# An earlier first weight chunk, other pauses around an inverse, and one bank for the last sums in a single-core layer

## The chip, the cores and the metric

The kernel runs on one core of one Trainium2 chip. Five engines of the core take part: TensorE (PE in the profile) multiplies matrices, VectorE (DVE), ScalarE (ACT) and GpSimd (POOL) work on tiles, and SyncE (SP) sends DMAs. ScalarE sends DMAs too, from a queue of its own. Each engine takes its instructions in a fixed order, and a wait stops what stands behind it on the same engine. The metric is the time of one execution on the device in microseconds. Before the change it is 2013.53 us, the median of three runs (2012.96 to 2017.21).

## The reference

One layer is computed for 256 prompt tokens and 8 single-token samples, 264 columns in all (T), at a model width of 2048 (16 tiles of 128):

```
x = x + 0.5 * swiglu(rmsnorm(x), gate1, up1, down1)     # width 5504 = 43 tiles
p = rmsnorm(x) @ w_in                                   # 38 tiles of 128 columns
mix = [ rwkv7(p[r, k, v, w, a, g]), attention(p[q, k, v]) ]   # 16 heads of 64 each
x = x + mix @ w_out
x = x + 0.5 * swiglu(rmsnorm(x), gate2, up2, down2)
y = rmsnorm(x)
```

The RWKV part runs a recurrence over the tokens, `S = S*decay - (S kk)(kk a)^T + v k^T`. The attention part is a window of 128 with a sink and a relative bias; the samples use cached keys and values. States and new cache rows are outputs beside y.

## The kernel before

**Weights.** Each weight matrix comes as chunks of 128 x 512 in float32. `chunk()` (L116) makes a raw tile by DMA on SP (256 KB; six raw buffers), then a rounded copy hi on ScalarE (L123) and lo = raw - hi on VectorE (four buffers each). TensorE takes hi and lo in `gemm` (L127): per 128 x 128 block three matmuls of 264 columns, hi by the high part of the activations, hi by their low part, lo by the high part, so 12 per chunk. There are 1288 chunks: 1 to 536 are the first feed-forward part, 537 to 688 w_in, then w_out and the second feed-forward part. The numbers of chunks in the prediction count these.

**The start.** Ten matmuls on a tile of ones (NWARM) run before any data is there. `first_ffn` (L285 on) loads x0 (the norm's gains and tile 0 of x) and the next tiles of x on ScalarE's queue; `load(k)` splits tile k into its high and low part. In the first part of `ffn` eight banks are filled in turns of four k-tiles.

**The mixing stage.** The w_in product runs over 38 tiles with `tick` after every chunk (and the w_out product too). A tick advances all living tasks by one step; tasks are generators, and `pause(n)` lets n ticks pass. So the program's order interleaves small work with chunks. A planner (the tile framework with a timeline of its own) then fixes each engine's order from that, with the chunks' casts and subtractions at high priority, and it may move work past other work of the same engine. RWKV runs in four batches of two head pairs. `prep` makes the scaled keys, gates and the masked products gm of a pair; `chain` (L521) does the rest of a batch:

1. blocks of gm go through DRAM (sa) to X and Y, 32 x 32 triangles (tile name Xt for Y), in the layout of L539 and L540;
2. `pause(DWAIT[i])`, then a 30-step inverse on VectorE, two small operations per step (st and Xt);
3. the inverse goes through DRAM again, sb by L557 and TT by L562, on SP;
4. `pause(DWAIT[i])`, then two VectorE transposes, TN (L567);
5. matmuls TN,gm, a ScalarE copy zs (L579), matmuls TT,zs, a copy into TT (L588), matmuls kr,TT, copies W (L602) and uv (L604);
6. matmuls of W, uv, and the recurrence of three S steps, each followed by VectorE updates Z and S; then y copied from the bank (L657) and from XD (L658), S sent out from ScalarE's queue (out_wkvp, L660), and a norm (matmuls y,C, squares, t,C, reciprocals L693).

```
yield from pause(DWAIT[bt.i])
for s in range(1, 31):
    ...
    tt(V, t, bc(X[:, s:s + 1, s + 1:], shp), bc(Y[:, :m, s:s + 1], shp), ALU.mult)
    tt(V, Y[:, :m, s + 1:], Y[:, :m, s + 1:], t, ALU.add)
...
yield from pause(DWAIT[bt.i])
TN = ring((P, n * 4, 32), "TN", 1)
```

Attention tasks (scores, softmax, the product with the values) start after the RWKV batches have been launched and run between the same chunks.

**The tail.** `second_ffn` collects squares of the finished x tiles into two sums. At the end matmuls turn each sum into a column of a bank (sm), two columns of three are added, a square root and a reciprocal follow, three matmuls spread the factor over 128 partitions (rp), ScalarE copies it to rb, and VectorE (from rp) and GpSimd (from rb) multiply the 16 tiles, each piece going out by DMA in turn on SP and ScalarE's queue (L952). Five matmuls into `hot` follow the sums.

Of the kernel before, what the change touches and what calls it, by code (L numbers as in the profile page):

```python
# [9 lines left out]
AF = mybir.ActivationFunctionType  # L10
ALU = mybir.AluOpType
# [16 lines left out]
CH, NRAW, NHL = 4, 6, 4  # L28
NACC, NM = 3, 5
NS, NO, NY, NH, NT, NLD = 38, 8, 8, 40, 16, 6  # L30
NWARM = 10
NGM, NKR, NUV, NTT, NBT = 10, 5, 3, 2, 5
NSTEP = 4
DWAIT = (8,8,8,4)
PW = (2, 1, 3, 2, 9)
ALPHA = math.exp(-0.5)
LKV = 26
# [10 lines left out]
def body(tc, I, O):  # L48
# [8 lines left out]
    def tt(e, out, a, b, op):  # L57
        return e.tensor_tensor(out=out, in0=a, in1=b, op=op)  # L58
# [8 lines left out]
    def act(out, in_, f, **k):  # L67
        return A.activation(out=out, in_=in_, func=f, **k)  # L68
# [4 lines left out]
    def mm(out, lhsT, rhs, start=True, stop=True, **k):  # L73
        TE.matmul(out, lhsT, rhs, start=start, stop=stop, **k)  # L74
# [20 lines left out]
    with ExitStack() as ctx:  # L95
# [17 lines left out]
        def mp():  # L113
            return pp.tile([P, 512], F32, tag="m", bufs=NM, name=uid("m"))
# [9 lines left out]
                tt(e, lo[:, :w], raw[:, :w], hi[:, :w].bitcast(F32), ALU.subtract)  # L124
            return hi, lo

        def gemm(ps, src, xs, step=None, rng=None, ahead=True):  # L127
            n = len(xs)
            for k0 in range(0, n, CH):
                k1 = min(n, k0 + CH)  # L130
                if rng and k0 not in rng:
                    continue
                hi, lo = chunk(src[:, k0 * P:k1 * P], k1 - k0, V, ahead)
                for k in range(k0, k1):
                    xh, xl = xs[k]
                    c = slice((k - k0) * P, (k - k0 + 1) * P)
                    mm(ps[:, :T], hi[:, c], xh, k == 0, False)
                    mm(ps[:, :T], hi[:, c], xl, False, False)
                    mm(ps[:, :T], lo[:, c], xh, False, k == n - 1)
                if step:  # L140
                    step()
# [65 lines left out]
            n, c, b = copies.pop()  # L207
            tc.keep_in_program_order(A.dma_start(O[n][b, 0:127, :], I[c][b, 1:128, :]))

        def ffn(nrm, xr, gu, dn, nxt, load, begin=None, side=None):  # L210
            rstd = None
            f0 = 0
            for pi, nf in enumerate(PARTS):
                hs = [None] * nf
                late = []
                if begin:
                    early(pi)
                first = pi == 0
                if first:
                    banks = [acc() for _ in range(NACC)] + [mp() for _ in range(NM)]  # L220
                    n0 = len(banks) // 2
                    for k in range(CH):
                        at = load(k)
                    for k0 in range(0, KD, CH):
                        if begin and k0 + CH < KD:
                            begin(k0 // CH + 1)
                        xs = nrm.xs + [None] * (KD - len(nrm.xs))
                        for i, ps in enumerate(banks):
                            with tc.issue_after(at.ins) if begin and k0 == 0 < i else nullcontext():
                                gemm(ps, gu[i // 2, i % 2], xs, rng=(k0,), ahead=False)  # L230
                            if i >= len(banks) - CH and k0 + CH < KD:
                                load(k0 + CH + i - len(banks) + CH)
                    for f in range(n0):
                        raw = [tmp(), tmp()]
                        V.tensor_copy(raw[0], banks[2 * f][:, :T])
                        A.copy(raw[1], banks[2 * f + 1][:, :T])
                        late.append((f, *raw))
                for f in range(f0 + n0 if first else f0, f0 + nf):
                    pgu = [acc(), acc()]
                    if first and f == n0:  # L240
                        sq = iter(range(KD))

                        def step():
                            for k in [x for _, x in zip(range(2), sq)]:
                                nrm.square(xr[k], k % 2, True)
                    else:
                        step = None
                    if begin and pi and copies:
                        copy_one()
                    if side and pi:  # L250
                        next(side, None)
                    for ps, w in zip(pgu, (gu[f, 0], gu[f, 1])):
                        gemm(ps, w, nrm.xs, step)
                    last = f == f0 + nf - 1
                    if rstd is None:
                        rstd = nrm.rstd(tmp())
                    late.append((f, *(x[:, :T] for x in pgu)))
                    now = [late.pop()]
                    for _ in range(len(late) if last else min(len(late), 2 if first and f == n0 + 1 else 1)):
                        now.append(late.pop(0))  # L260
                    for j, pg, pu in now:
                        E = V if last else G
                        g = tmp()
                        tt(V, g, pg, rstd, ALU.mult)
                        s = tmp()
                        act(s, g, AF.Silu)
                        u = tmp()
                        tt(V, u, pu, rstd, ALU.mult)
                        tt(E, u, u, s, ALU.mult)
                        hi, lo = tmp(dt=F32R), tmp(dt=F32R)  # L270
                        A.copy(hi, u)
                        tt(E, lo, u, hi.bitcast(F32), ALU.subtract)
                        hs[j - f0] = (hi, lo)
                if pi == len(PARTS) - 1:
                    nrm.xs = None
                for o in range(KD):
                    ps = acc()
                    gemm(ps, dn[o, :, f0 * P:(f0 + nf) * P], hs)
                    stt(xr[o], ps[:, :T], 0.5, xr[o], ALU.mult, ALU.add)
                    if pi == len(PARTS) - 1:  # L280
                        nxt(o)
                f0 += nf

        def first_ffn(n2):
            def load(k0):  # L285
                return n1.split(xr[k0], True)

            def nxt(o):
                n2.split(xr[o])
                n2.square(xr[o])  # L290
                A.dma_start(xsp[o], xr[o])

            with tc.tile_pool(name="f1", bufs=1) as fp:
                cur[0] = (fp, NH)
                x0 = fp.tile([P, KD + T], F32, name="x0")
                A.dma_start(x0, I["x0"])
                n1 = Norm(VG1, gains=x0[:, 0:KD])
                xr = [x0[:, KD:]]
                for j0, j1 in ((1, 2), (2, 4)):
                    xg = fp.tile([P, j1 - j0, T], F32, name=uid("x"))  # L300
                    A.dma_start(xg, I["xT"][:, j0:j1, :])
                    xr += [xg[:, j] for j in range(j1 - j0)]

                def more(q):
                    xg = fp.tile([P, 4, T], F32, tag="x", bufs=3, name=uid("x"))
                    tc.keep_in_program_order(A.dma_start(xg, I["xT"][:, q * 4:q * 4 + 4, :]))
                    xr.extend(xg[:, j] for j in range(4))

                ffn(n1, xr, I["gu1"], I["dn1"], nxt, load, more)

        def dec_state(fp, XR):
            n = 4
# [599 lines left out]
        def second_ffn(n3, xr, XR):  # L912
# [6 lines left out]
            with tc.tile_pool(name="f2", bufs=1) as fp:  # L919
# [11 lines left out]
                ffn(n3, xr, I["gu2"], I["dn2"], nxt, load, None, side)  # L931
                assert next(side, side) is side
                p = fin.sums[0]
                sm, rp, hot = [mp(), mp()], mp(), mp()
                for m, q in zip(sm, p):
                    for j in range(3):
                        mm(m[0:88, j:j + 1], q[:, j * 88:j * 88 + 88], ones[:, 0:1])
                for _ in range(5):
                    mm(hot[:, :P], ones, p[1][:, :P])
                A.copy(rt[:, 3:6], sm[0][0:88, 0:3])  # L940
                tt(V, rt[:, 0:3], sm[1][0:88, 0:3], rt[:, 3:6], ALU.add)
                act(rt[:, 0:3], rt[:, 0:3], AF.Sqrt, scale=1.0 / D, bias=eps[0:88, 0:1])
                V.reciprocal(rt[:, 0:3], rt[:, 0:3])
                for j in range(3):
                    mm(rp[:, j * 88:j * 88 + 88], bc(rt[:, j:j + 1], (88, P)), C[0:88, CID:CID + 88])
                rb = tmp()
                A.copy(rb, rp[:, :T])
                for i, (e, o, n) in enumerate(((V, 0, 1), (V, 1, 1), (G, 2, 1), (V, 4, 4), (G, 3, 1), (V, 8, 4), (G, 14, 1), (V, 12, 2), (V, 15, 1))):
                    y = ys[o // 4][:, o % 4:o % 4 + n]
                    r = rb if e is G else rp[:, :T]  # L950
                    tt(e, y, y, bc(r.unsqueeze(1), (P, n, T)), ALU.mult)
                    (SP, A)[i % 2].dma_start(O["yT"][:, o:o + n, :], y)  # L952
# [109 lines left out]
```

## Time and profile before

| | before |
|---|---|
| median of 3 runs (lowest, highest) | 2013.53 us (2012.96, 2017.21) |
| the profiled execution's time | 2014.05 us |
| its span | 2012.1 us |
| mean granted TensorE clock | 0.997 |
| TensorE busy | 1990.5 us (99%) |
| VectorE busy | 1306.4 us (65%) |
| ScalarE busy | 1032.6 us (51%) |
| GpSimd busy | 257.0 us (13%) |
| DMA moved | 358.39 MB, 178 GB/s over the span |

Rows of a timeline begin with the start and the length in us; then stand the engine, the line, the operation, out<-in, the shape and the number of merged instructions; in square brackets, the idle time before and what released it. Matmul records count twice for float32 operands (ten matmuls are twenty rows). In the answers on waits there are the total, the number and the longest, in us. PEclk is the share of full clock that TensorE was granted.

### The profile page before, as it was taken

Reading aid. Unit: us, or ns where it says so; the run is one execution under the profiler, and the core shown is the slowest. Engines: PE = TensorE matmul, PEld = TensorE weight load, DVE = VectorE, ACT = ScalarE, POOL = GpSimd, SP = SyncE. Lnnn points to the kernel's source line nnn. Section 1 sums busy time; section 2 is a strip of 40 time slices with the busy share of each in tenths; the row PEclk is TensorE's granted clock in tenths of the full one; section 3 lists DMA queues with packets and bytes.
Section 4 is the critical chain, followed back from the end, with each engine's and each line's share of the span. In section 5 each row is a group of like instructions: output and inputs, shape, how many; then the busy total and the mean of one; then the engine's idle time right before and its main releaser. Section 6 shows DMA issues by size and latency. Waiting matters only on the chain.

```text
span 2012.1 us, 45443 instructions
## 1 busy us (share of the span) xinstructions
PE 1990.5 (99%) x17088; PEld 1956.4 (97%) x17088; DVE 1306.4 (65%) x2576; ACT 1032.6 (51%) x2047; POOL 257.0 (13%) x368
## 2 busy tenths in 40 slices
PE   9999999999999999999998999999999999999998
PEld 9999999999999999999988889999999999999998
DVE  5865555655556577688777766776666666666665
ACT  5644444444444456655555654654444444444445
POOL 0401001010010222121200010120101001010012
PEclk9999999999999999999999999999999999999999
DMA  6565565655555566554555345565565665655554
GB/s 226 177 192 193 183 194 189 185 184 176 187 177 185 182 200 211 153 157 129 149 150 165 118 137 181 174 184 184 192 179 191 187 192 189 185 191 184 191 179 145
DMA packets 227708, 358.39 MB, mean 178 GB/s; under 512 B 42384, under 2 KB 81312, under 8 KB 227488
## 3 DMA queue, kind: packets, MB, share of 16 engines
q1 hardware_dynamic: 220896, 346.41, 55.0%
q10 hardware_dynamic: 6592, 9.08, 1.4%
q8 instruction: 134, 2.20, 0.4%
q14 instruction: 86, 0.70, 0.1%
HBM read 347.26 MB, written 10.21 MB: 178 GB/s over the span
## 4 chain that ended last, share of the span: by engine, by line
PE 94%; DMA 2%; DVE 2%; issue 1%; ACT 1%; SPq 1%; DVEq 0%; POOL 0%; ACTq 0%; POOLq 0%
PE acc L74 85%; PE m L74 8%; DMA sb<-Xt 1%; DVE lo L58 0%; DMA TT<-sb 0%; DMA xsp<-x 0%; DMA x<-in_x 0%; DMA Xt<-sa 0%; PE m L507 0%; ACT t L68 0%; DVE y L58 0%; DMA sa<-gm 0%; SPq L557 0%; ACT hi L123 0%; PE m L757 0%
## 5 line engine op out<-in xcount | busy, mean ns | idle before, releaser
L58 DVE TENSOR_TENSOR lo<-raw,hi 128x512 fp32r<-128x512 f32 (+1 forms) x1288 | 871.2, 680 | 547.9 <-ACT hi L123 521.1
L123 ACT CAST hi<-raw 128x512 fp32r<-128x512 f32 (+1 forms) x1288 | 777.1, 607 | 840.9 <-PE acc L74 762.3
L74 PE MATMUL acc<-s,hi 128*128 128x264 f32 x5940 | 1112.0, 287 | 0.9 <-ACT hi L123 0.9
L74 PEld LDWEIGHTS acc<-s,hi 128*128 128x128 f32 x5940 | 924.2, 189 | 6.7 <-issue 1.9
L74 PE MATMUL acc<-s,lo 128*128 128x264 f32 x2970 | 848.9, 286 | 4.1 <-DVE lo L58 3.9
L74 PEld LDWEIGHTS acc<-s,lo 128*128 128x128 f32 x2970 | 560.3, 189 | 8.0 <-DVE lo L58 5.4
L74 PE MATMUL acc<-t,hi 128*128 128x264 f32 x2752 | 502.6, 284 | 0.0
L74 PEld LDWEIGHTS acc<-t,hi 128*128 128x128 f32 x2752 | 426.0, 188 | 0.0
L74 PE MATMUL acc<-t,lo 128*128 128x264 f32 x1376 | 388.6, 284 | 0.0
L58 POOL TENSOR_TENSOR t<-t,t 128x264 f32<-128x264 f32 (+1 forms) x148 | 150.9, 1020 | 1148.3 <-ACT hi L123 790.8
L74 PEld LDWEIGHTS acc<-t,lo 128*128 128x128 f32 x1376 | 258.3, 188 | 0.0
L74 PE MATMUL acc<-y,hi 128*128 128x264 f32 x648 | 123.7, 284 | 0.0
L74 PEld LDWEIGHTS acc<-y,hi 128*128 128x128 f32 x648 | 100.9, 188 | 0.1
L74 PE MATMUL acc<-y,lo 128*128 128x264 f32 x324 | 91.7, 283 | 0.0
L58 DVE TENSOR_TENSOR t<-acc,t 128x264 f32<-128x264 f32 x156 | 67.4, 432 | 36.8 <-PE acc L74 36.5
L58 POOL TENSOR_TENSOR o<-o,o 128x264 f32<-128x264 f32 x43 | 36.4, 847 | 234.6 <-ACT o L68 228.9
L74 PE MATMUL acc<-o,hi 128*128 128x264 f32 x324 | 63.1, 285 | 0.0
L74 PEld LDWEIGHTS acc<-y,lo 128*128 128x128 f32 x324 | 61.0, 188 | 0.0
L61 DVE SCALAR_TENSOR_TENSOR s<-acc,s 128x264 f32<-128x264 f32 x96 | 40.6, 427 | 15.4 <-PE acc L74 14.9
L74 PEld LDWEIGHTS acc<-o,hi 128*128 128x128 f32 x324 | 50.3, 188 | 0.0
L74 PE MATMUL m<-s,hi 128*128 128x264 f32 x260 | 48.0, 284 | 0.0
L61 DVE SCALAR_TENSOR_TENSOR x<-acc,x 128x264 f32<-128x264 f32 x96 | 40.5, 426 | 9.8 <-PE acc L74 9.3
(249 smaller groups left out, 1278.8 us busy)
## 6 DMA issues: line engine op xcount, KB each, us to landing
raw<-in_gu SPq DMA_DIRECT2D x688, 256.0 KB, 3.3
raw<-in_dn SPq DMA_DIRECT2D x224, 256.0 KB, 2.8
raw<-in_win SPq DMA_DIRECT2D x152, 256.0 KB, 3.4
raw<-in_dn SPq DMA_DIRECT2D x160, 192.0 KB, 2.7
raw<-in_wout SPq DMA_DIRECT2D x64, 256.0 KB, 3.2
xsp<-x ACTq DMA_DIRECT2D x16, 132.0 KB, 3.7
s<-xsp SPq DMA_DIRECT2D x16, 132.0 KB, 4.2
ld<-in_sT SPq DMA_DIRECT2D x16, 128.0 KB, 3.5
```

The source lines that it names most:

```text
L58: return e.tensor_tensor(out=out, in0=a, in1=b, op=op)
L61: return V.scalar_tensor_tensor(out=out, in0=a, scalar=s, in1=b, op0=op0, op1=op1)
L74: TE.matmul(out, lhsT, rhs, start=start, stop=stop, **k)
L123: A.copy(hi[:, :w], raw[:, :w])
```

## The change

There are three parts. At the start, one more warm-up matmul is made; tile 0 of x is split and the first weight chunk (raw, hi, lo) is made before the other tiles of x are asked for; and the load of tiles 2 and 3 of x (264 KB) goes to SP's queue, behind that first chunk's, instead of being the third on ScalarE's. `gemm` and `ffn` take the ready chunk. In the mixing stage, the pauses of `chain`, which stand both ahead of the inverse and between its end and the transposes, are 10, 10, 10 and 2 instead of 8, 8, 8 and 4. At the tail, the six matmuls of the two sums add into one bank, so that the copy and the addition are gone; there are three hot matmuls instead of five; the factor for GpSimd comes from a second bank with three matmuls of its own; and the 16 tiles are cut into eight pieces instead of nine, with two for GpSimd (tiles 8 and 12) instead of three (2, 3 and 14).

```diff
-NWARM = 10
+NWARM = 11
-DWAIT = (8,8,8,4)
+DWAIT = (10,10,10,2)
...
-        def gemm(ps, src, xs, step=None, rng=None, ahead=True):
+        def gemm(ps, src, xs, step=None, rng=None, ahead=True, ready=None):
...
-                hi, lo = chunk(src[:, k0 * P:k1 * P], k1 - k0, V, ahead)
+                hi, lo = ready or chunk(src[:, k0 * P:k1 * P], k1 - k0, V, ahead)
...
-                    for k in range(CH):
+                    for k in range(len(nrm.xs), CH):
                         at = load(k)
...
-                                gemm(ps, gu[i // 2, i % 2], xs, rng=(k0,), ahead=False)
+                                gemm(ps, gu[i // 2, i % 2], xs, rng=(k0,), ahead=False, ready=ready)
+                            ready = None
...
-                for j0, j1 in ((1, 2), (2, 4)):
+                at = load(0)
+                with tc.issue_after(at.ins):
+                    first = chunk(I["gu1"][0, 0][:, 0:CH * P], CH, V, False)
+                for e, j0, j1 in ((A, 1, 2), (SP, 2, 4)):
                     xg = fp.tile([P, j1 - j0, T], F32, name=uid("x"))
-                    A.dma_start(xg, I["xT"][:, j0:j1, :])
+                    e.dma_start(xg, I["xT"][:, j0:j1, :])
...
-                sm, rp, hot = [mp(), mp()], mp(), mp()
-                for m, q in zip(sm, p):
+                sm, rp, hot = mp(), mp(), mp()
+                for i, q in enumerate(p):
                     for j in range(3):
-                        mm(m[0:88, j:j + 1], q[:, j * 88:j * 88 + 88], ones[:, 0:1])
-                for _ in range(5):
+                        mm(sm[0:88, j:j + 1], q[:, j * 88:j * 88 + 88], ones[:, 0:1], i + j == 0, i == 1, skip_group_check=True)
+                for _ in range(3):
                     mm(hot[:, :P], ones, p[1][:, :P])
-                A.copy(rt[:, 3:6], sm[0][0:88, 0:3])
-                tt(V, rt[:, 0:3], sm[1][0:88, 0:3], rt[:, 3:6], ALU.add)
-                act(rt[:, 0:3], rt[:, 0:3], AF.Sqrt, scale=1.0 / D, bias=eps[0:88, 0:1])
+                act(rt[:, 0:3], sm[0:88, 0:3], AF.Sqrt, scale=1.0 / D, bias=eps[0:88, 0:1])
                 V.reciprocal(rt[:, 0:3], rt[:, 0:3])
...
-                rb = tmp()
-                A.copy(rb, rp[:, :T])
-                for i, (e, o, n) in enumerate(((V, 0, 1), (V, 1, 1), (G, 2, 1), (V, 4, 4), (G, 3, 1), (V, 8, 4), (G, 14, 1), (V, 12, 2), (V, 15, 1))):
+                rb, again = tmp(), mp()
+                for j in range(3):
+                    mm(again[:, j * 88:j * 88 + 88], bc(rt[:, j:j + 1], (88, P)), C[0:88, CID:CID + 88])
+                A.copy(rb, again[:, :T])
+                for i, (e, o, n) in enumerate(((V, 0, 1), (V, 1, 1), (V, 2, 2), (V, 4, 4), (G, 8, 1), (V, 9, 3), (G, 12, 1), (V, 13, 3))):
```

More of the change, by code (lines that the diff above doesn't have):

```diff
@@ L208, in copy_one, with ffn @@
             tc.keep_in_program_order(A.dma_start(O[n][b, 0:127, :], I[c][b, 1:128, :]))
-        def ffn(nrm, xr, gu, dn, nxt, load, begin=None, side=None):
+        def ffn(nrm, xr, gu, dn, nxt, load, begin=None, side=None, ready=None):
             rstd = None
@@ L307, in more @@
                     xr.extend(xg[:, j] for j in range(4))
-                ffn(n1, xr, I["gu1"], I["dn1"], nxt, load, more)
+                ffn(n1, xr, I["gu1"], I["dn1"], nxt, load, more, None, first)
         def dec_state(fp, XR):
```

## The prediction

> **What bounds the kernel now.** I read the page first, then the waits of TensorE, then the timeline around each wait. The page says that little but TensorE can be shortened:
>
> ```profile
> span 2012.1 us, 45443 instructions
> PE 1990.5 (99%) x17088; PEld 1956.4 (97%) x17088; DVE 1306.4 (65%) x2576; ACT 1032.6 (51%) x2047; POOL 257.0 (13%) x368
> ```
>
> Only some 21 us of the span are without a matmul. No part of the change removes a large matmul, so it can only move those 21 us, or the speed at which matmuls run. The waits of TensorE (line, releaser, total, times, longest) say where they are:
>
> ```profile
> PE acc L74 <- DVE lo L58: 3.9, 3, 2.2
> PE m L74 <- ACT zs L579: 3.5, 1, 3.5
> PE m L74 <- ACT W L602: 1.4, 1, 1.4
> PE m L74 <- DVE TN L567: 0.5, 1, 0.5
> ```
>
> All four lie in the mixing stage, where the pauses work. The largest, in the timeline of TensorE, with the ScalarE copy that ends it and the same matmuls of an undisturbed batch (914):
>
> ```profile
> 1094.14 0.69 PE L74 MATMUL m<-TN,gm 32*32 32x32 f32 x32
> 1098.29 1.45 PE L74 MATMUL m<-TT,zs 32*32 32x32 f32 x32 [3.45 <-ACT zs L579]
> 1101.25 3.73 PE L74 MATMUL m<-kr,TT 64*64 64x128 f32 x32
> ...
> 1097.87 0.75 ACT L579 COPY zs<-m 32x256 f32<-32x256 f32 x2
> ...
> 914.42 1.97 PE L74 MATMUL m<-kr,TT 64*64 64x128 f32 x32
> ```
>
> The reader sees a stop of 3.45 us in batch 3, then matmuls at nearly twice their time (3.73 against 1.97). The windows show why (columns: window, length, five engines, PEclk, DMA share, GB/s):
>
> ```profile
> 1098.00:1102.00 4.00, 3.56 (x48) 3.00 (x49) 1.82 (x9) 2.78 (x10) 0.00 (x0) 0.58 1.04 343
> 1102.00:1106.00 4.00, 4.00 (x34) 3.67 (x32) 2.53 (x12) 3.99 (x16) 0.74 (x1) 0.56 0.89 284
> 1037.80:1044.00 6.20, 6.17 (x62) 5.80 (x64) 6.20 (x13) 3.14 (x6) 2.14 (x5) 1.00 0.63 167
> ```
>
> For 8 us the clock was 0.57, which costs 8 x 0.43 = 3.4 us; after a stop of 2.20 in batch 2, at 1037, it stayed at 1.00. Batch 3 thus pays 3.45 + 3.4 = 6.9 us.
>
> **The pauses, batch 3 (4 to 2).** In the instruction order of the changed kernel the last inverse step of batch 3 stands after lo 682 (chunks counted from the start), the transposes after lo 686 and 688, and ScalarE copies zs before the softmax's exponentials instead of behind them. Between TN,gm and TT,zs stand about 20 weight matmuls. The 6.9 us go. Late next are W and uv, whose copies stand behind casts and softmax work; the nearest row is the W wait of 1.4. I take 2.0 for new waits (bounds 0 and 6.9): **-4.9**.
>
> **The pauses, batches 0 to 2 (8 to 10).** Here the pause stands twice, ahead of the inverse and between its end and the transposes. But it counts chunks as the program is written, and the planner puts the transposes nearer: the inverse of batch 1 ends after lo 623 and both transposes stand between lo 624 and 625; in batch 2 the end is after lo 652, the transposes on both sides of the work behind lo 655; in batch 0 the end is after lo 608, the transposes behind lo 611 (before: 612 and 613). What the way through DRAM takes, from VectorE's timeline of batch 1 and batch 2:
>
> ```profile
> 944.25 0.16 DVE L58 TENSOR_TENSOR Xt<-Xt,st 128x8 f32<-128x8 f32 x1
> ...
> 952.65 0.43 DVE L567 STREAM_TRANSPOSE TN<-TT 32x256 f32<-32x256 f32 x1 [2.16 <-DMA TT<-sb]
> ...
> 1023.05 0.17 DVE L58 TENSOR_TENSOR Xt<-Xt,st 128x8 f32<-128x8 f32 x1
> ...
> 1033.76 0.43 DVE L567 STREAM_TRANSPOSE TN<-TT 32x256 f32<-32x256 f32 x1 [2.47 <-DMA TT<-sb]
> ...
> 1037.83 0.40 PE L74 MATMUL acc<-s,lo 128*128 128x264 f32 x1 [2.20 <-DVE lo L58]
> ```
>
> From the end of the inverse to the first transpose it is 8.4 us (952.65 - 944.25) or 10.7, and the transpose was waiting already. While it waits, VectorE makes no lo, and TensorE has at most four chunks in hand. The prices for the rest, from the page (lo, in ns) and the timelines:
>
> ```profile
> L58 DVE TENSOR_TENSOR lo<-raw,hi 128x512 fp32r<-128x512 f32 (+1 forms) x1288 | 871.2, 680 | 547.9 <-ACT hi L123 521.1
> ...
> 912.82 0.62 ACT L123 CAST hi<-raw 128x512 fp32r<-128x512 f32 x1 [0.55 <-PE acc L74]
> 914.28 0.62 ACT L123 CAST hi<-raw 128x512 fp32r<-128x512 f32 x1 [0.85 <-PE acc L74]
> ...
> 915.70 0.21 DVE L58 TENSOR_TENSOR st<-X,Xt 128x50 f32<-128x50 f32 x1
> 919.52 1.79 DVE L422 RECIPROCAL t<-m 128x264 f32<-128x264 f32 x1
> ...
> 925.96 1.07 ACT L458 COPY uv<-m 64x128 f32<-64x128 f32 x4 [0.66 <-PE m L455]
> 935.21 0.34 ACTq L660 DMA_DIRECT2D out_wkvp<-S  x1
> 936.62 0.61 PE L74 MATMUL m<-y,C 128*128 128x264 f32 x2
> ...
> 953.13 0.37 ACT L510 COPY BT<-m 128x256 f32<-128x256 f32 x1 [0.21 <-PE m L507]
> 953.51 0.74 ACT L512 COPY BT<-m 64x256 f32<-64x256 f32 x2
> ```
>
> A chunk is 1.46 us (914.28 - 912.82). Batches 0 and 1 meet at chunks 617 to 625; I count from the end of the second S step on TensorE, in 617, as 0.
> First wait: before the update that the third S step needs (chunk 619), VectorE now has 12 inverse operations (2.5), two mask multiplies and lo 621 of 512 columns (2.0) and some five small ones (0.9, an estimate at 0.2 each): ready at 5.4 less the 0.6 that the second step itself takes, 4.8. TensorE is there after two chunks, 2.9: **1.9**.
> Second wait: TensorE reaches the second y,C in chunk 621 at 4.8 + 3.8 = 8.6 (two chunks and 0.9 of small work after the step). The last S is ready at 7.7 (lo 622 and ten small operations later), and ScalarE's queue now holds, ahead of the second y<-XD copy, the DMA issue of S that waits for it (0.34), four kr copies (1.07), one of 0.37, another issue (0.34) and three BT copies (1.1): 11.1. **2.5**.
> Third wait: the inverse ends at 9.8 (0.2 + lo 623 + six steps after that S), so TN is at 18.2 at the soonest; with 0.43, a reciprocal of 1.79 between the transposes, the second transpose 0.43 and lo, lo 625 is there at 21.5 to 22. TensorE goes on at 11.1, has the rest of 621 and 622 to 624 (5.7) and some nine small matmuls at 0.3 (2.7), and wants lo 625 at 19.7: **2.2**.
> Together 6.6 where the old order lost 0.2 (the waits of lo, 3.9 in three, less batch 2's 2.2, lie elsewhere): **+6.4**. Bounds: 0, if TensorE is itself late by these few us, and 11 if lo 621 comes late too.
> Batch 2 has the same ScalarE order in chunk 651 while y,C stands in 649: the same count gives 3.0. Its transposes hold lo 656: the inverse ends 9.4 after its third S step, TN is 8.4 to 10.7 later, two reciprocal-sized pieces and small ones (3.6) follow to lo 656: 22 to 24 against TensorE's 19.5, 2.5 to 4.5, say 3.1 where it was 2.2. **+3.9** (bounds -2.2 and +7).
> Batch 0: TN,gm stands 1.7 chunks earlier, 2.5 us; the row shows 0.5 now and VectorE's spare time takes part: 1.5. **+1.0** (0 to 2.5).
>
> **The start.** The first chunk, x0 and the loads, in the timeline:
>
> ```profile
> 0.99 4.63 PE L74 MATMUL m<-ones 128*128 128x128 f32 x20 [0.99 <-POOL eps L150]
> 6.56 0.81 PE L74 MATMUL acc<-s,hi 128*128 128x264 f32 x2 [0.94 <-ACT hi L123]
> 7.95 0.51 ACT L68 ACTIVATE s<-x,x 128x264 fp32r<-128x264 f32 x1 [1.02 <-DMA x<-in_xT]
> 12.73 0.64 PE L74 MATMUL acc<-s,hi 128*128 128x264 f32 x2
> 13.33 0.40 PE L74 MATMUL m<-s,hi 128*128 128x264 f32 x2
> ```
>
> SP takes the 264 KB of xT[2:4] between the first weight chunk and the second, ScalarE's queue loses it, and ScalarE no longer waits 1.02 for it. The eleventh warm-up matmul costs 4.63 / 10 = 0.46 (the ten are 20 rows) inside the 0.94 of waiting. Behind it, raw 1 and later come 0.6 later on SP; six chunks in hand hide that. **-1.0** (bounds +0.3, and -3 if the half-speed pairs, 0.64 against 0.40, end one stretch earlier).
>
> **The tail.**
>
> ```profile
> 2000.61 0.63 PE L74 MATMUL m<-ones,o 128*88 128x1 f32 x6 [0.65 <-ACT o L68]
> 2001.10 1.36 PE L74 MATMUL m<-o,ones 128*128 128x128 f32 x10
> 2001.34 0.16 DVE L58 TENSOR_TENSOR rt<-m,rt 88x3 f32<-88x3 f32 x1 [1.30 <-PE m L74]
> 2003.13 0.38 ACT L947 COPY t<-m 128x264 f32<-128x264 f32 x1 [1.30 <-PE m L74]
> 2003.54 4.05 DVE L58 TENSOR_TENSOR y<-y,m 128x264 f32<-128x264 f32 x6 [1.51 <-ACT t L947]
> 2003.59 2.14 POOL L58 TENSOR_TENSOR y<-y,t 128x264 f32<-128x264 f32 x3 [4.70 <-ACT t L947]
> ```
>
> The sum of two banks goes (0.16). VectorE need not wait for the copy (2003.54 - 2003.13 = 0.4). Each of five hot matmuls is 0.27 (1.36 / 5); two fewer count where the factor's matmuls stand behind them, and I count half, 0.3. Against these 0.9, GpSimd starts later behind three more matmuls and its copy, with two tiles instead of three, and the last piece is three tiles (396 KB) where it was one: 0.4. I take **-0.5** (bounds -0.9, and +0.5 if that last transfer is the end).
>
> **Sum.** -1.0 - 0.5 + 1.0 + 6.4 + 3.9 - 4.9 = +4.9. The profiled run took 2014.05 (1.95 around its span), 0.52 above the median of three, 2013.53; from the median it is 2018.4. I call a change under 0.2% (4.0 us) none, about what this kernel's measurement can tell.
>
> **Rivals.**
> A, the forecast: new waits in batches 0 to 2 exceed what batch 3 saves. 2016 to 2022; 0.40, of which 0.10 below 2017.6.
> B, faster: TensorE, not VectorE, is behind at each end of the inverse, so that VectorE is four chunks ahead when it meets the transposes. Four chunks and their small matmuls are 5.8 + 2.7 = 8.5, as much as the 8.4 of the loads: it decides if VectorE has that lead at lo 624 and 655. Batch 1 before speaks for it (VectorE waited 2.16, TensorE not at all), batch 2 against it. Then only batch 3's saving and the ends count, with 0 to 2 of small waits: 2013.5 - 1.5 - 6.9 + 1.0 = 2006. 0.25.
> C, slower still: the new stops cut the clock as at 1098. There 3.45 us did it, while the 2.20 of batch 2 left it at 1.00. Stops of 3 and 3.1 are near that; one more such loss gives 2018.4 + 3.4 = 2022, two 2025. 0.17. The Trainium skill, "TensorE: Matmul & The Clock Gate", section "Why this matters for your kernels", says to leave no idle gap of TensorE over about 3 us, since an idle window halves the clock; by that rule the stops of 3.0 and 3.1 would both be charged and the time be 2025. The trace agrees for 3.45.
> D, the pauses do nothing net: half of the waits are hidden, 2018.4 - 5 = 2013. 0.18, nearly all within 0.2%.
> So faster 0.26 (B and a little of D), within 0.2% 0.27, slower 0.47. Range 2006 to 2026.
>
> **What would show it.** TensorE's waits of the changed kernel: zs gone and PEclk 1.00 near 1094; waits for lo, for y's copy and for S between 915 and 945, and two in batch 2; VectorE's wait of TN for TT<-sb above its total of before. At the start, no wait of ScalarE for xT; at the tail, VectorE's first product some 0.7 us nearer to the last square. Wrong, if TensorE waits under 3 us in batches 0 to 2, or if a half-clock stretch remains after batch 3's transposes.

## The result, and the profile after

The changed kernel takes 1998.72 us, the median of five runs (1997.52 to 2000.81), against 2013.53 before (2008.44 to 2017.21, five runs). The ratio is 0.9929, with a 95% interval from 0.9912 to 0.9947: some 14 us less, where 5 us more were forecast. The forecast range began at 2006.

The head of the page of the changed kernel:

```profile
span 1996.9 us, 45460 instructions
PE 1983.0 (99%) x17092; PEld 1952.0 (98%) x17092; DVE 1305.6 (65%) x2575; ACT 1030.9 (52%) x2046; POOL 258.6 (13%) x367
```

and its waits of TensorE (line, releaser, total, times, longest):

```profile
PE m L74 <- DVE TN L571: 1.2, 1, 1.2
PE acc L74 <- DVE lo L58: 1.0, 4, 0.3
PE m L74 <- DVE y L58: 0.4, 1, 0.4
PE acc L74 <- POOL s L58: 0.3, 1, 0.3
```

TensorE stands still for 13.9 us (21.6 before), and is busy for 7.5 us less with the same large matmuls. The waits for zs, for W and the 2.2 us for lo are gone. (Lines behind the start have moved by three or four: L571 is the old L567.)

Three reciprocals (L194) stand at the same place of the work in both kernels: the norm of the first feed-forward part, the norm ahead of w_in, and that of the second feed-forward part. Their rows in the timeline of VectorE cut the span into stages. Before:

```profile
71.04 1.80 DVE L194 RECIPROCAL t<-t 128x264 f32<-128x264 f32 x1 [0.63 <-ACT t L68]
...
774.47 1.80 DVE L194 RECIPROCAL rs<-rs 128x264 f32<-128x264 f32 x1 [1.03 <-ACT rs L68]
...
1304.66 1.80 DVE L194 RECIPROCAL t<-t 128x264 f32<-128x264 f32 x1 [0.48 <-ACT t L68]
```

and after:

```profile
67.94 1.80 DVE L194 RECIPROCAL t<-t 128x264 f32<-128x264 f32 x1 [0.62 <-ACT t L68]
...
771.29 1.80 DVE L194 RECIPROCAL rs<-rs 128x264 f32<-128x264 f32 x1 [1.02 <-ACT rs L68]
...
1290.78 1.80 DVE L194 RECIPROCAL t<-t 128x264 f32<-128x264 f32 x1 [0.43 <-ACT t L68]
```

The start gives 3.1 us (71.04 - 67.94), the rest of the first feed-forward part 0.1, the stretch with the mixing stage 10.7 (530.19 to 519.49), and what follows 1.3 (707.44 to 706.12). The sum is the 15.2 us of the two spans. In the mixing stage TensorE stands still for 2.8 us where it stood for 9.8; the other 3.7 us of the 10.7 are time in which it was busy.

**The mixing stage.** The last step of the inverse and the first transpose of batch 1 (931) and of batch 3 (1068), with batch 3's matmuls, in the timelines of VectorE and TensorE of the changed kernel:

```profile
931.62 0.17 DVE L58 TENSOR_TENSOR Xt<-Xt,st 128x8 f32<-128x8 f32 x1
...
938.12 0.43 DVE L571 STREAM_TRANSPOSE TN<-TT 32x256 f32<-32x256 f32 x1 [3.13 <-DMA TT<-sb]
...
1068.92 0.17 DVE L58 TENSOR_TENSOR Xt<-Xt,st 128x8 f32<-128x8 f32 x1
...
1077.86 0.43 DVE L571 STREAM_TRANSPOSE TN<-TT 32x256 f32<-32x256 f32 x1 [3.68 <-DMA TT<-sb]
1078.34 0.24 PE L74 MATMUL m<-TN,gm 32*32 32x32 f32 x2 [1.16 <-DVE TN L571]
...
1088.49 1.96 PE L74 MATMUL m<-kr,TT 64*64 64x128 f32 x32
```

Batch 3 now costs 1.16 us and keeps its clock (kr,TT takes 1.96, not 3.73). VectorE does wait for a transpose, 3.13 and 3.68 us, as was forecast; but TensorE does not come to a stop behind it in batch 1.

**The start.** The first matmul into a bank of tag m in TensorE's timeline of the changed kernel:

```profile
10.26 0.41 PE L74 MATMUL m<-s,hi 128*128 128x264 f32 x2
```

It runs at 10.26, at 13.33 before: the stretch of pairs that took 0.64 is not there.

**The tail.** VectorE's first product and the sums ahead of it:

```profile
1985.59 0.63 PE L74 MATMUL m<-ones,o 128*88 128x1 f32 x6 [0.64 <-ACT o L68]
1987.71 4.33 DVE L58 TENSOR_TENSOR y<-y,m 128x264 f32<-128x264 f32 x6 [0.99 <-PE m L74]
```

The product starts 2.12 after the last sums, 2.93 before, and from those sums to the end of the span it is 11.3, against 11.5: VectorE's 0.8 is lost again behind it, for from the first product to the end of the span it is 9.2, against 8.6.

### The profile page after: what moved, and what is told of

It is laid out like the page before. It is cut to its first block, busy times and chain, and to the rows that moved or that the text cites. A ratio compares the mean times of both kernels' runs of the same rounds, so it can differ in the third digit from the quotient of the medians.

```text
span 1996.9 us, 45460 instructions
## 1 busy us (share of the span) xinstructions
PE 1983.0 (99%) x17092; PEld 1952.0 (98%) x17092; DVE 1305.6 (65%) x2575; ACT 1030.9 (52%) x2046; POOL 258.6 (13%) x367
## 4 chain that ended last, share of the span: by engine, by line
PE 97%; DMA 1%; DVE 1%; issue 0%; ACT 0%; SPq 0%; POOL 0%; DVEq 0%; ACTq 0%; POOLq 0%
PE acc L74 87%; PE m L74 9%; DVE lo L58 0%; PE m L511 0%; DMA TT<-sb 0%; DMA xsp<-x 0%; DMA sb<-Xt 0%; DMA x<-in_x 0%; DVE y L58 0%; DMA Xt<-sa 0%; PE m L761 0%; PE m L498 0%; DMA ld<-in_g 0%; PE m L763 0%; PE m L762 0%
## 5 line engine op out<-in xcount | busy, mean ns | idle before, releaser
L61 DVE SCALAR_TENSOR_TENSOR s<-acc,s 128x264 f32<-128x264 f32 x96 | 40.6, 427 | 15.5 <-PE acc L74 15.1
```

What stands on the lines that cost most here:

```text
L61: return V.scalar_tensor_tensor(out=out, in0=a, scalar=s, in1=b, op0=op0, op1=op1)
```

## The experiments

Each is the kernel before with a part of the change, or the changed kernel with one number moved. The ratios are to the kernel before, in runs of the same chip.

**The start alone.**

```diff
-NWARM = 10
+NWARM = 11
...
+                at = load(0)
+                with tc.issue_after(at.ins):
+                    first = chunk(I["gu1"][0, 0][:, 0:CH * P], CH, V, False)
+                for e, j0, j1 in ((A, 1, 2), (SP, 2, 4)):
```

> The kernel before with the start part alone (eleven warm-up matmuls, first chunk made ahead, tiles 2 and 3 of x on SP's queue). Theory 1 (each part acts by itself, and the sum of the parts is the change): the full-speed pairs begin about 3 us earlier, at about 10.3 instead of 13.3, and the time falls by 3.0 us (2 to 4); the waits of the mixing stage stay as they were before, zs 3.5, lo of batch 2 2.2, W 1.4. Theory 2 (an earlier start shifts the loads of the mixing stage against each other and that also takes away waits there): the time falls by 5 us or more, and the 1.5 us wait for lo near 858 is gone in this run too. Theory 3 (when the clock is released is a matter of chance from run to run): the median falls by under 1 us and the full-speed pairs begin at different times in different runs.

Measured: 2016.37 us, 1.0003 [0.9990, 1.0016]. The first stage is 3.4 us shorter (its reciprocal stands at 67.66), so theory 3 falls for the start itself; the wait for lo near 858 is still there (1.48 at 854), so theory 2 falls too; but the whole is no faster, which theory 1 did not foresee. The mixing stage of this profile took 541.0 us. Its planner order differs from that of before only around batch 3 and in w_out, and there TensorE waits for a ScalarE cast behind the softmax; the waits for W in batches 1 and 2, whose order is the old one, are larger than in the profile of before as well (1.41 at 987 and 2.03 at 1065, where before has 1.38 at 1064 alone). The wait for that cast:

```profile
1107.36 0.63 PE L74 MATMUL acc<-s,hi 128*128 128x264 f32 x3 [1.87 <-ACT s L891]
```

**The tail alone.** The edit is the last part of the change.

```diff
-                sm, rp, hot = [mp(), mp()], mp(), mp()
+                sm, rp, hot = mp(), mp(), mp()
...
-                A.copy(rb, rp[:, :T])
+                A.copy(rb, again[:, :T])
```

> The kernel before with the tail alone. Both theories: within 1 us of before (the two profiles differ by 0.2 us from the last squares' matmuls to the end); VectorE's first product starts about 0.7 us nearer to those matmuls, and the output ends at the same distance from them.

Measured: 2017.00 us, 1.0009 [0.9999, 1.0018]: nothing, as expected. This run taught something else. Up to the tail its instruction order is that of before, instruction by instruction, and yet its mixing stage took 536.2 us where the profile of before had 530.2: the waits for W are 5.0 us in four places here and 1.4 in one there. So the old order is one that loses a varying amount in this stage. The profile on which the prediction was made shows one of its smaller losses there, though as a whole (2014.05) it is near the medians of the kernel before, 2013.53 to 2015.51 in four sets of runs.

**The pauses alone.**

```diff
-DWAIT = (8,8,8,4)
+DWAIT = (10,10,10,2)
```

> The kernel before with the pauses 10, 10, 10, 2 alone. Theory 1: about 10 us less (9 to 12): the zs wait 3.5 and the half-clock stretch 3.4 behind it, lo of batch 2 2.2 and W 1.4 are gone, about 1.2 of a wait for a transpose comes. Theory 2: only batch 3's 7 us come from the pauses, and the waits of batch 2 stay unless the start is changed as well. The prediction's account would make it slower by 6 us.

Measured: 2003.27 us, 0.9945 [0.9933, 0.9957], 11 us less: theory 1. Its order in the mixing stage is that of the changed kernel but for a few VectorE operations near 925, its mixing stage 521.8 us, and the waits for zs and W are gone.

**The last pause alone.**

```diff
-DWAIT = (8,8,8,4)
+DWAIT = (8,8,8,2)
```

> The kernel before with the last pause alone, 8, 8, 8, 2. Theory 1: batch 3's wait for zs and the half clock go, 5 to 7 us less; the waits of batch 2 (lo 2.2, W 1.4) stay. If the waits of batch 2 go here too, the last pause moves them by way of the planner and the first three pauses are not needed.

Measured: 2015.90 us, 1.0006 [0.9995, 1.0017]. The zs wait is still 3.5 us. Both expectations fall: with the other pauses as before, the inverse of batch 3 still ends after lo 687, and its zs copies still stand behind the softmax.

**The first three pauses alone.**

```diff
-DWAIT = (8,8,8,4)
+DWAIT = (10,10,10,4)
```

> The kernel before with the first three pauses alone (10, 10, 10, 4). The instruction order of batches 0 to 2 is then the changed kernel's, while batch 3's zs copies stand behind three more casts and after the softmax (after hi 692 where the changed kernel has 690). Theory 1: 11 us less as with all four pauses if batch 3 is cured by being early; some 6 us less, with the zs wait still there, if the last pause of 2 is what puts zs ahead of the softmax once the others have moved.

Measured: 2014.82 us, 0.9995 [0.9984, 1.0006]. Neither number was met. Batches 0 to 2 have the good order (inverses after lo 623 and 652), but batch 3 eats the gain, in a way that neither theory named. Batch 3 in the timelines of VectorE and TensorE of this run:

```profile
1083.19 0.17 DVE L58 TENSOR_TENSOR Xt<-Xt,st 128x8 f32<-128x8 f32 x1
...
1094.11 0.43 DVE L567 STREAM_TRANSPOSE TN<-TT 32x256 f32<-32x256 f32 x1 [2.46 <-DMA TT<-sb]
1094.60 0.24 PE L74 MATMUL m<-TN,gm 32*32 32x32 f32 x2 [2.69 <-DVE TN L567]
...
1097.40 1.06 PE L74 MATMUL m<-TN,gm 32*32 32x32 f32 x30 [2.56 <-DVE TN L567]
```

and the windows over it (window, length, five engines, PEclk, DMA share, GB/s):

```profile
1096.00:1100.00 4.00, 2.14 (x36) 1.86 (x38) 1.13 (x2) 0.73 (x2) 0.00 (x0) 0.57 0.79 235
1100.00:1104.00 4.00, 3.55 (x52) 3.10 (x51) 1.61 (x9) 2.13 (x9) 0.00 (x0) 0.50 0.85 242
1104.00:1108.00 4.00, 4.00 (x54) 3.79 (x52) 1.86 (x7) 3.75 (x14) 0.77 (x2) 0.65 0.62 172
```

From the end of the inverse to the first transpose it is 10.9 us (1094.11 - 1083.19), for the planner put raw weight loads between the DMAs of sb and TT on SP; two stops of 2.6 us follow, and 12 us at about half clock. That is what the forecast feared for batches 1 and 2; it is real, at another place.

**Batch 0's pause alone.**

```diff
-DWAIT = (8,8,8,4)
+DWAIT = (10,8,8,4)
```

> The kernel before with 10 instead of 8 for batch 0 alone (10, 8, 8, 4). In its instruction order the inverse of batch 1 ends after lo 623 as in the changed kernel (628 before), that of batch 2 after 657 (652 and 661). Theory 1 (the gain comes from the planner putting the inverses of batches 1 to 3 earlier, which the pause of batch 0 brings about by itself): 6 us less or more, TensorE's waits at 1037 and 1064 for lo and W gone. Theory 2 (each batch's pause removes its own wait): under 2 us less, the waits of batches 1 to 3 stay.

Measured: 2008.42 us, 0.9969 [0.9958, 0.9979], 6 us less: theory 1 in size, though not in detail. The lo wait in batch 2 is 1.1 and the W wait does not go, it is 3.42 in this profile. The profiled execution took 2014.02 us, the slowest of twelve, so its waits are those of a bad case; but it shows well what makes W late. First VectorE's rows, then ScalarE's and TensorE's:

```profile
1055.28 0.19 DVE L58 TENSOR_TENSOR st<-X,Xt 128x30 f32<-128x30 f32 x1 [7.03 <-DMA Xt<-sa]
1058.16 0.41 DVE L604 COPY uv<-m 64x256 f32<-64x256 f32 x1
1058.60 0.37 ACT L604 COPY uv<-m 64x256 f32<-64x256 f32 x1 [5.68 <-DVE uv L604]
1059.00 0.32 ACT L602 COPY W<-m 128x192 f32<-128x192 f32 x1
1059.37 0.48 PE L74 MATMUL m<-BT,W 64*64 64x64 f32 x4 [3.42 <-ACT W L602]
```

The first step of the next batch's inverse stands in VectorE's order ahead of this batch's uv copy, and waits 7.03 us for its X and Xt. ScalarE's uv copy waits for VectorE's, W stands behind it, and TensorE waits for W.

**Start and pauses, without the tail.** The start's edit as above, and the pauses:

```diff
-NWARM = 10
+NWARM = 11
-DWAIT = (8,8,8,4)
+DWAIT = (10,10,10,2)
...
+                    first = chunk(I["gu1"][0, 0][:, 0:CH * P], CH, V, False)
```

> Start part and pauses together, tail as before. Its order up to the tail is the changed kernel's. If the start is worth its 3 us once the mixing stage's order is the same, 1999 to 2000, 3 to 4 us below the pauses alone; if the start gives nothing on the median (as it did alone), 2003.

Measured: 2001.58 us, 0.9932 [0.9917, 0.9947]. Its order up to the tail is the changed kernel's, and its first reciprocal stands at 67.95, as there. The step from the pauses alone, 0.9945 to 0.9932, is 2.6 us, a little under the 3 to 4 expected, and the intervals overlap; that the start is shorter is shown by the stages of the profiles, not by these ratios.

**Which half of the start.** First the eleventh warm-up matmul with the pauses:

```diff
-NWARM = 10
+NWARM = 11
-DWAIT = (8,8,8,4)
+DWAIT = (10,10,10,2)
```

> Pauses 10, 10, 10, 2 and the eleventh warm-up matmul, with the loads and the first chunk as before. The instruction order past the start is that of the pauses alone (2003.3, 0.9945 of before). Theory 1 (the eleventh matmul keeps TensorE busy long enough, so that the full clock comes earlier): full-speed pairs begin at about 10 as with the whole start part (9.9 to 10.3 in four profiles; 11.0 to 13.3 in six with ten matmuls), and the time is that of start and pauses, 2001. Theory 2 (the data do it): they begin at 11 to 13, and the time stays at 2003.

and its counterpart, the first chunk and the moved load with ten warm-up matmuls and the pauses (the tail as before in both):

```diff
-DWAIT = (8,8,8,4)
+DWAIT = (10,10,10,2)
...
+                    first = chunk(I["gu1"][0, 0][:, 0:CH * P], CH, V, False)
+                for e, j0, j1 in ((A, 1, 2), (SP, 2, 4)):
```

> The counterpart: the first chunk made ahead and tiles 2 and 3 on SP's queue, with ten warm-up matmuls, and the pauses. Theory 2: full-speed pairs begin at about 10, the time 2001. Theory 1: at 11 to 13, the time 2002 to 2003, with only the 1.0 of ScalarE's wait for xT gained.

Measured: 2003.65 (0.9939 [0.9918, 0.9959]) and 2001.59 (0.9929 [0.9907, 0.9950]). The first matmul into a bank of tag m runs at 12.57 in the first and at 10.02 in the second: theory 2, the first chunk and the moved load do it (which of the two was not separated), and the eleventh matmul alone does nothing that shows here; the two ratios overlap and decide nothing. Over all profiles, it runs at 9.88 to 10.26 in the seven with the new loads and at 10.96 to 13.33 in the seven with the old. TensorE's rows at the start of the run with the pauses alone (old loads):

```profile
6.93 0.39 PE L74 MATMUL acc<-s,lo 128*128 128x264 f32 x1 [0.22 <-DVE lo L58]
...
8.16 1.12 PE L74 MATMUL acc<-s,hi 128*128 128x264 f32 x2 [0.32 <-ACT s L68]
```

the same run's window over the stretch that follows:

```profile
8.00:12.00 4.00, 3.70 (x16) 3.50 (x17) 3.40 (x6) 2.59 (x6) 0.00 (x0) 0.57 0.90 292
```

and that window of the run with the first chunk made ahead and ten warm-up matmuls:

```profile
8.00:12.00 4.00, 4.00 (x35) 4.00 (x34) 3.01 (x5) 2.03 (x4) 0.00 (x0) 1.00 1.02 373
```

With the old loads TensorE waits at 8 us for the split of tile 2 (0.32 here, behind the 0.81 and 0.22 for hi and lo), and a stretch at 0.57 of the clock follows. With the new loads the tile is there and the clock stays, in all seven profiles. That the stop itself brings the clock down is not shown, for the run with the last pause alone, with the old loads, has the same three stops (1.11, 0.22 and 0.30) and keeps its clock:

```profile
8.00:12.00 4.00, 3.86 (x29) 3.66 (x30) 3.65 (x7) 3.02 (x6) 0.00 (x0) 1.00 0.94 303
```

This run shows what the wait is worth by itself. Its first matmul into a bank of tag m is the one at 10.96, and its first reciprocal stands at 68.75, 0.8 to 1.1 us behind those of the seven runs with the new loads (67.66 to 67.95); in the other six with the old loads it stands 2.3 to 3.8 behind. So the wait is the forecast's 1 us, and the clock makes it 3 in most executions. In the profile of before the clock did not fall but came late: the very first pair, at 6.56, takes 0.81, where the runs with the pauses and with the last pause alone have 0.51. Its windows print a PEclk of 1.00 there all the same, since its trace has no record of the clock ahead of 13.2 us; the lengths of the pairs are what to read.

**Longer and shorter pauses in the changed kernel.** First two more:

```diff
-DWAIT = (10,10,10,2)
+DWAIT = (12,12,12,2)
```

> The changed kernel with pauses 12, 12, 12, 2. If longer pauses go on moving the inverses and their transposes apart, no transpose wait of TensorE is left and the time is 1 to 2 us below the changed kernel's; if the order was good by chance, it is slower by 2 us or more.

then one more:

```diff
-DWAIT = (10,10,10,2)
+DWAIT = (11,11,11,2)
```

> The changed kernel with pauses 11, 11, 11, 2. In its order the inverses end earlier still (after lo 618, 644 and 673 instead of 623, 652 and 682). If an earlier chain is what makes the kernel faster, 1996 to 1998 and no transpose wait in batch 3; if what counts is how the chain meets the other work (as 12, 12, 12, 2 showed with 2021), it is slower than the changed kernel's 1999 to 2000.

then one less:

```diff
-DWAIT = (10,10,10,2)
+DWAIT = (9,9,9,2)
```

> The changed kernel with pauses 9, 9, 9, 2: inverses end after lo 625, 649 and 682, the transposes three chunks later (628, 652, 687), near the changed kernel's. An order so near should give 1998 to 2004 if the distance to the transposes and the end of the inverse decide, and may be anywhere between 1998 and 2020 if single copies at the meeting of two batches decide.

Measured: 2021.32 (1.0027 [1.0015, 1.0039]), 2024.41 (1.0049 [1.0031, 1.0067]) and 2012.86 (0.9989 [0.9976, 1.0002]). No neighbour of 10, 10, 10, 2 keeps its gain. With 11 the chain is earliest and the kernel slowest. The largest of TensorE's waits in that run, from its timeline, ends among VectorE's inverse steps (st):

```profile
997.86 0.69 PE L74 MATMUL m<-N,PT 64*64 64x64 f32 x8 [4.58 <-DVE st L58]
```

An earlier chain is therefore not better by itself. With 9 the waits are many and small, 0.2 to 1.9 us in some fifteen places, though the inverses end within three chunks of the changed kernel's: single copies at the meeting of two batches may decide, but which do is not shown.

Moving the pause ahead of the inverse alone, or the one ahead of the transposes alone, was not tried for all four batches at once. What each of the two pauses does by itself is thus argued from the rows and not measured apart.

## Why the prediction was wrong, point by point

**Batch 3, -4.9: right for the four pauses together.** The zs wait and the half clock behind it go, and 1.16 us of a new wait comes: -3.45 - 3.4 + 1.16 = -5.7, where the 3.4 is by the clock and was not measured apart. But the step credited it to the pause of 2, and alone that pause does nothing (1.0006): the gain comes only with the other pauses, which put the chain of batch 3 earlier (its inverse ends after lo 682, not 687).

**Batches 0 and 1, +6.4: wrong, and the main fault.** TensorE's waits there are 0.36 and 0.28 us at 943 and 948, and 0.33 in batch 0. None of the three waits counted was there. (By its own terms TensorE wants lo 625 at 11.1 + 5.7 + 2.7 = 19.5, not 19.7; that changes nothing.) In batch 0, where +1.0 was forecast, the 0.49 for TN went.
- The first wait set the count's zero at the end of the second S step and supposed that VectorE's update began with it. The update S stands at 921.73 and TensorE's second step at 923.59: VectorE was 1.9 us ahead. The update that the third step needs began at 926.86, and the third step ran at 927.32 without a wait, 3.1 us after the end of the second where 4.8 were forecast.
- The second wait was a misreading of names. The y<-XD copy behind the BT copies writes the y of the *next* batch. With buffer numbers left out, it looked like the one that y,C needs:

```profile
931.44 0.61 PE L74 MATMUL m<-y,C 128*128 128x264 f32 x2
...
932.70 0.20 ACT L662 COPY y<-XD 128x8 f32<-128x8 f32 x1
```

The matmul runs before the copy that it was said to wait for.
- The third wait took 8.4 us through DRAM from batch 1 of before. It is 6.5 here (938.12 - 931.62). On SP, two loads of in_sT stood between sb and TT before:

```profile
945.25 2.91 SPq L557 DMA_DIRECT2D sb<-Xt  x4
948.26 2.23 SPq L346 DMA_DIRECT2D ld<-in_sT  x2
950.78 0.82 SPq L562 DMA_DIRECT2D TT<-sb  x2
```

In the changed kernel only one raw load does:

```profile
931.86 2.55 SPq L561 DMA_DIRECT2D sb<-Xt  x4
934.50 0.55 SPq L122 DMA_DIRECT2D raw<-in_win  x1
935.92 1.81 SPq L566 DMA_DIRECT2D TT<-sb  x4
```

So what rival B described happened in batch 1: TensorE had enough work in hand for the way through DRAM, since that way was shorter. Its time, 2006, is still 7 us too long, for it kept the old waits of batch 2. The range of this cost ran from 8.4 to 10.7 by the rows of before, and the changed kernel's 6.5 and 7.7 lie below it (8.9 in batch 3).

**Batch 2, +3.9: wrong.** The same misread copy stood there, and the first transpose met no wait of VectorE at all (0 to 1.3 us in the six profiles with this order in batch 2); the old 2.2 for lo and 1.4 for W went away instead, -3.6.

**What the prediction left out: the pause ahead of the inverse.** It priced the second pause only, and called the W wait of batch 2 the nearest row for a new cost. The waits of VectorE for the first step of an inverse (st, which reads X and Xt and waits for their loads, whichever DMA the row names) are long before and shorter after. The first steps of batches 1, 2 and 3 before:

```profile
912.23 0.19 DVE L58 TENSOR_TENSOR st<-X,Xt 128x30 f32<-128x30 f32 x1 [4.29 <-DMA ld<-in_sT]
...
985.15 0.19 DVE L58 TENSOR_TENSOR st<-X,Xt 128x30 f32<-128x30 f32 x1 [2.77 <-DMA ld<-in_sT]
...
1060.16 0.19 DVE L58 TENSOR_TENSOR st<-X,Xt 128x30 f32<-128x30 f32 x1 [5.00 <-DMA out_vp<-s]
```

and after:

```profile
905.21 0.19 DVE L58 TENSOR_TENSOR st<-X,Xt 128x30 f32<-128x30 f32 x1 [1.91 <-DMA Xt<-sa]
...
973.23 0.19 DVE L58 TENSOR_TENSOR st<-X,Xt 128x30 f32<-128x30 f32 x1 [2.06 <-DMA Xt<-sa]
...
1043.05 0.19 DVE L58 TENSOR_TENSOR st<-X,Xt 128x30 f32<-128x30 f32 x1 [3.33 <-DMA Xt<-sa]
```

They sum to 12.1 us before and 7.3 after. It is no accident of two profiles: the four with the old order at these places (before, the start alone, the tail alone, the last pause alone) have 12.1 to 16.0, the five with the four new pauses 7.3 to 8.4. Such a wait blocks what stands behind it on VectorE, and through uv and W it reaches TensorE: the run with batch 0's pause shows the whole path, and the trace of before had it too, behind the 5.00 at 1060, on ScalarE and then on TensorE:

```profile
1063.48 0.37 ACT L604 COPY uv<-m 64x256 f32<-64x256 f32 x1 [3.64 <-DVE uv L604]
...
1064.24 0.33 PE L74 MATMUL m<-BT,W 64*64 64x64 f32 x4 [1.38 <-ACT W L602]
```

These waits are not the whole account. With pauses of 11 they sum to 7.1 us, and that kernel is the slowest, by other waits. In batch 0 the first step stands behind lo 586 in every run and its wait went from 5.00 to 2.91; it lies in a part of the order that the change leaves alone, and TensorE's wait behind it, 1.49 us at 858 before and none after, is between 0 and 1.5 us in different runs. I do not count it as won, though the 10.7 us of the two profiles contain it.

**The start, -1.0: the direction right, the term mis-sized.** It measures -3.1 between these two profiles, at the lower bound given, which had been set for just this case. The step priced the wait, some 1 us, and not the clock, which makes up the rest.

**The tail, -0.5: nearly nothing.** 0.2 us between the profiles, nothing in the ratio.

**Rival C** (half clock from stops of 3 us) did not come, as the stops did not. It came in the run with the first three pauses, from two stops of 2.69 and 2.56 us with 0.24 us of matmuls between them, and in the run with batch 0's pause behind its stop of 3.42 (0.50 from 1058 to 1062).

**What stays open.** Why a pause that is longer lets the planner finish the inverses of batches 1 and 2 earlier (lo 628 to 623 and 661 to 652); that batch 0's pause alone starts it is shown (0.9969), how is not. Why 10 is better than 9, 11 and 12. Why the clock at the start is kept in one run with the old loads and not in the others. And why the start alone, 3.4 us shorter in its stage, gains nothing on the median: its batch 3 order costs part of it, the rest may lie in the spread of the old order, which is argued and not shown.

## What to carry to other kernels

A pause in a program that a planner reorders is not a delay of known length: read where each engine's order puts the waiting instruction against the DMA that it needs, for every pause and not only the one at the end, and follow who is queued behind it. Follow copies by buffer number before calling one late. And take a second execution of the kernel before: here two executions of one instruction order differ by 6 us in one stage, so a cost read from a single profile may be its lucky case.

## What the runs showed of the hardware

The length of a stop alone does not say here whether the clock falls. At 1037 the 2.20 us of the kernel before left it at 1.00, while 1.81 us at the same place in the run with the last pause alone were followed by 0.57 (1038 to 1042). In the first microseconds a stop of 0.32 us was followed by 0.57 (8 to 12) in the run with the pauses alone, one of 0.30 by 1.00 in the run with the last pause alone. The Trainium skill, "TensorE: Matmul & The Clock Gate", section "Why this matters for your kernels", asks for no idle gaps over about 3 us; by that rule neither the 1.81 nor the 0.32 would have cost the clock, and the traces do not agree with it there. The Trainium skill, on the same page, section "A second HAM failure mode: psum-queue depth-cycling", says that frequent short idling can also make the clock swing. That fits the three stops at 5 to 8 us of the run with the pauses alone, and not those of the run with the last pause alone, which kept its clock. In the clock records of the traces the dips between 100 us and the end of the work last 3.41 us, or two or three times that: 6.83 us at 1098.67 in the kernel before and at 1178.88 in the changed one.

The clock also falls with no stop before it. In the changed kernel's windows, where attention's matmuls of 8 columns run between small ones, TensorE is busy all the time, by the record, until the clock goes down:

```profile
1174.00:1177.00 3.00, 3.00 (x30) 2.67 (x29) 1.12 (x2) 0.94 (x2) 0.00 (x0) 1.00 0.63 198
1177.00:1180.00 3.00, 3.00 (x25) 2.60 (x26) 1.03 (x4) 0.84 (x3) 0.37 (x3) 0.81 0.17 60
1180.00:1183.00 3.00, 2.72 (x15) 2.09 (x12) 1.56 (x3) 2.71 (x9) 2.82 (x9) 0.50 0.14 44
1183.00:1186.00 3.00, 3.00 (x16) 3.00 (x16) 1.49 (x2) 0.13 (x2) 1.20 (x2) 0.55 0.00 0
```

By the clock that is 3 x (0.19 + 0.50 + 0.45) = 3.4 us lost. The profile of before has 1.00 at the same work (1180 to 1195), and so has the run with the first chunk made ahead and ten warm-up matmuls; the other twelve, the changed kernel's among them, have the dip. So it is a matter of the execution, not of the change. It costs less than 3.4: that run has the changed kernel's order here, and the same matmuls take it 15.5 us (from 1171.92) where the changed kernel takes 17.4 (from 1169.78), 1.9 less; without the dip TensorE waits 0.51 and 0.67 us there for ScalarE and GpSimd.
